# A filter transform as one float32 matmul per tile in place of three float32r matmuls

## The chip, the cores and the metric

The kernel runs on one core of a Trainium2 chip. Its metric is device time in microseconds (us), the median of several runs. The engines are TensorE (PE in the profile, its weight loads PEld), VectorE (DVE), ScalarE (ACT), GpSimd (POOL) and SyncE (SP), which issues nearly all transfers. Each executes its own instructions in order and waits on semaphores for the others.

## What is computed

One layer of an encoder for two sequences, of 512 and 2048 rows: a normalised input times w_in, three groups of heads (mLSTM, retention, Hyena), and a product with w_out. The change concerns the Hyena group's filters, which depend on the weights alone:

```python
hid = jnp.sin(fr * (feats @ w1 + b1))
hid = jnp.sin(fr * (hid @ w2 + b2))
filt = (hid @ w3).reshape(l, HY_ORDER, 2, HY_WIDTH)
filt = filt * jnp.exp(-t[:, :, None, None] * jnp.abs(deltas))
fwd, bwd = filt[:, :, 0], filt[:, :, 1]
two_sided = jnp.concatenate([fwd[:1] + bwd[:1], fwd[1:], jnp.zeros_like(fwd[:1]), jnp.flip(bwd[1:], axis=0)], axis=0)
two_sided = two_sided / jnp.sum(jnp.abs(two_sided), axis=0, keepdims=True)
spec = jnp.fft.rfft(two_sided, axis=0)
...
y = jnp.fft.irfft(jnp.fft.rfft(u, n=2 * l, axis=1) * spec[None], n=2 * l, axis=1)[:, :l]
```

The kernel does each Fourier transform of length 2l in two steps, over n1 and then over n2, each a matmul with a constant matrix.

## The kernel before

A float32 product of full accuracy is made here of three passes on parts: `split` writes hi, a copy of the source rounded to a narrower type, on ACT, and lo, the source less hi, on DVE (or POOL); `mm3` accumulates hi x hi, hi x lo and lo x hi in one PSUM tile. For the projections with w_in the parts are float16 (lines 540 and 550); for filters and transforms they are float32r, a type in which PE reads four bytes and makes a single pass (lines 372 to 374). The profile writes float32r operands of a matmul as f32, and as fp32r where ACT and DVE write them.

The filters come in two rounds, order 0 and order 1, of 40 tiles of 128x512 each (8 tiles for the short sequence, 32 for the long one). `filters(o)` is a loop over tiles n in which several steps of different tiles are put one behind the other: `first(n)` multiplies the hidden layer hd by w3 (three float32r matmuls into ps) and makes the window win on ACT; every fourth tile it also splits the next 128x512 of hd. `product(n)` writes f = ps x win on DVE. One turn later, `total` takes |f| on ACT and adds it to acc on POOL, and `second` splits f in f0 (ACT) and f1 (DVE). One turn after that, `third` multiplies by FA, the matrix of the DFT over n1 (three float32r matmuls), and `store` copies the result to fo on DVE and sends it to F in HBM. For the last tile of each filter (j = 0), `second` first adds a term for the skip to one row of f, which needs the finished sum acc (line 673) and so ends the chain of POOL. `filter_setup` loads the two FA matrices and splits them once.

The filter loop is a generator that is merged with others by planned costs: order 0 with the second half of the first Hyena projection, its gates and the end of the sine layers (`filter_mlp`, whose `h` is the first sine's result), order 1 with the Hyena projection of x1 and, on another stream, the Hyena transforms: `stage_a0` (parts hp, matrix ai) and `freq(0)` (parts hp, matrix cB, buffers hb). The generators give the program's sequence; a scheduler of the tile framework with its own simulated timeline then places the instructions of each engine. Tile pools set how many tiles of a name exist: f has FB = 1 buffer, win, fo, f0 and f1 have two. Line 660 is the product, 665 and 666 the sum, 694 the copy to fo; 365 and 366 are split's two rows for whatever tile, so tiles are told apart by name.

Of the kernel before, what the change touches and what calls it, by code (L numbers as in the profile page):

```python
# [10 lines left out]
F32R = mybir.dt.float32r  # L11
# [25 lines left out]

WK = 2
LF, LA, LI, LT, W1, W2, W3, LN, LM = 2.7, 2.5, 4.2, 1.6, 0.8, 1.08, 1.03, 1.5, 3.5
HB, HP, CB, FB, B1, B2, KA, KB, KC, LS2, WF, VB, FH = 9, 8, 3, 1, 5, 6, 3, 3, 1, 3, 70, 4, 8  # L40
R1, R2, R3, R4, M1, WG, W4, W5, W6 = 2.5, 2.0, 1.5, 0.6, 0.6, 60, 18, 11.5, 5.3


def geo(L):
    N = 2 * L
    N1 = N // 64
    V = N1 // 2
    return dict(N=N, N1=N1, K1=N1 // 2, V=V, GF=128 // N1, GS=128 // V, NTF=N // 128, NTS=L // 128)
# [98 lines left out]
class Trunk:  # L147
# [418 lines left out]
    def filter_setup(self):  # L566
        nc, C, p0 = self.nc, self.C, self.p0
        self.tneg = self.T(p0, [128, 40], "tneg", bufs=1)
        nc.sync.dma_start(self.tneg, C['tneg'])
        self.fa = {}  # L570
        for L in (LP, LS):
            self.fa[L] = [self.T(p0, [128, 128], f"FA{L}{i}", F32R, bufs=1) for i in range(2)]
            raw = self.T(p0, [128, 512], "fo")[:, 0:128]
            nc.sync.dma_start(raw, C[f'FA{L}'])
            self.split(*self.fa[L], raw)

    def filter_weights(self, o):
        nc, I, p0 = self.nc, self.I, self.p0
# [45 lines left out]
    def filters(self, o):  # L624
        nc, p0 = self.nc, self.p0
        w3, dl = self.filter_weights(o)
        tneg, fa = self.tneg, self.fa
        yield 3.0
        seq = [(L, 4 * b + t, t0 + 4 * b + t, i, t) for i, (L, b, t0) in enumerate(self.filter_blocks()) for t in reversed(range(4))]
        accs, hids, raws, st, sk = {}, {}, {}, {}, {}  # L630

        def fetch(i):
            raws[i] = self.T(p0, [128, 4, 128], "hd", bufs=1)
            nc.sync.dma_start(raws[i], self.hid[i].rearrange("p (t c) -> p t c", t=4))

        def first(n):
            L, j, jt, i, t = seq[n]
            if L not in accs:
                accs[L] = self.T(p0, [128, 512], "acc", bufs=1)
                nc.gpsimd.memset(accs[L], 0.0)  # L640
            if t == 3:
                if i == 0:
                    fetch(0)
                hids[i] = self.split(*(self.T(p0, [128, 4, 128], f"hd{x}", F32R, bufs=1) for x in range(2)), raws.pop(i))
                hids.pop(i - 1, None)
            if t == 2 and n + 4 < len(seq):
                fetch(i + 1)
            if j == 0:
                sk[L] = self.T(p0, [128, 512], "fo")[0:1]
                nc.sync.dma_start(sk[L], self.I['hy_skip'][:, o])  # L650
            ps = self.ps()
            self.mm3(ps, [x[:, t] for x in hids[i]], w3)
            win = self.T(p0, [128, 512], "win")
            nc.scalar.activation(win, dl, AF.Exp, scale=tneg[:, jt:jt + 1])
            st[n] = [ps, win]

        def product(n):
            ps, win = st[n]
            f = self.T(p0, [128, 512], "f", bufs=FB)
            nc.vector.tensor_tensor(out=f, in0=ps, in1=win, op=ALU.mult)  # L660
            st[n] = [f, win]

        def total(n):
            (f, win), acc = st[n], accs[seq[n][0]]
            nc.scalar.activation(win, f, AF.Abs)  # L665
            nc.gpsimd.tensor_tensor(out=acc, in0=acc, in1=win, op=ALU.add)  # L666

        def second(n):
            L, j, _, _, _ = seq[n]
            f, acc = st[n][0], accs[L]  # L670
            if j == 0:
                ps = self.ps()
                nc.tensor.matmul(ps[0:1], self.ones[:, 0:1], acc, start=True, stop=True)
                nc.vector.tensor_tensor(out=ps[0:1], in0=ps[0:1], in1=sk[L], op=ALU.mult)
                nc.vector.tensor_tensor(out=f[0:1], in0=f[0:1], in1=ps[0:1], op=ALU.add)
                ps = self.ps()
                for cb in range(4):
                    nc.tensor.matmul(ps[:, cb:cb + 1], acc[:, cb * 128:(cb + 1) * 128], self.ones[:, 0:1], start=True, stop=True)
                nc.vector.reciprocal(self.rs[L][:, o], ps[:, 0:4])
            else:  # L680
                total(n)
            st[n] = self.split(*(self.T(p0, [128, 512], f"f{x}", F32R) for x in range(2)), f)

        def third(n):
            L = seq[n][0]
            ps = self.ps()
            self.mm3(ps, fa[L], st[n])
            st[n] = ps

        def store(n):  # L690
            L, j, _, _, _ = seq[n]
            g = geo(L)
            fo = self.T(p0, [128, 512], "fo")
            nc.vector.tensor_copy(fo, st.pop(n))
            nc.sync.dma_start(self.F[L, o][:, j::g['NTF'], :], fo)

        n = len(seq)
        for i in range(n + 2):
            if i < n:
                first(i)  # L700
            if 0 <= i - 2:
                third(i - 2)
            if 0 <= i - 1 < n:
                if seq[i - 1][1] == 0:
                    total(i - 1)
                    yield self.lag(0.0, LS2, 1.28)
                second(i - 1)
            if 0 <= i - 2:
                store(i - 2)
            if i < n:  # L710
                product(i)
            yield self.lag(1.28, LT)
# [1022 lines left out]
```

## Time and profile before

| | |
|---|---|
| median of 3 runs | 2742.09 us (2740.89 to 2746.55) |
| the profiled execution's own time | 2752.46 us |
| its span, first to last instruction | 2750.7 us |
| PE busy (17,670 matmul records) | 2554.4 us, 93% |
| DVE busy | 1708.6 us, 62% |
| ACT busy | 1401.0 us, 51% |
| POOL busy | 758.2 us, 28% |
| mean granted clock of PE | 0.977 |

The busy times are of one profiled execution, whose time lies 10 us above the median. PE's matmuls overlap in the pipeline, so PE's busy time counts more than its work, and the distance from one start to the next says more about a matmul's price than its own duration does. The shares are means over stages that differ: the first filter round runs from about 157 to 404 us, the second to about 655 us, the Hyena transforms, further projections and retention to about 1690 us, and mLSTM and the output product behind that. The granted clock is a share of 2.4 GHz and has two levels, 2.4 and 1.2 GHz.

### The profile page before, as it was taken

The page shows a single profiled execution, that of the slowest core. Times are in us where ns is not written, and L with a number is a line of the kernel's source. Part 1 is how long each engine was busy: PE and PEld are TensorE (multiplying, and loading weights), DVE is VectorE, ACT ScalarE, POOL GpSimd, SP SyncE. Part 2 cuts the span into 40 slices and gives each one's busy share as a digit, 9 for nine tenths or more (in the row PEclk, how much of TensorE's full clock was granted, in tenths as well). Part 3 has the DMA queues.
Part 4 walks back from the last instruction along what each step waited for, and adds up shares of the span by engine and source line. Part 5 has one row for each costly group of instructions (what it writes and reads, how often), then busy time and mean ns, then how long its engine had stood idle before and what let it go on. Part 6 is the DMA issues. An engine that isn't in the chain of part 4 may idle for free.

```text
span 2750.7 us, 47623 instructions
## 1 busy us (share of the span) xinstructions
PE 2554.4 (93%) x17670; PEld 1927.4 (70%) x17670; DVE 1708.6 (62%) x3398; ACT 1401.0 (51%) x2710; POOL 758.2 (28%) x847
## 2 busy tenths in 40 slices
PE   7999979988998999988989998999999999899998
PEld 5556645544645788877777786787777877788887
DVE  7867768897786566576676666555566555622222
ACT  6456666765665465465665444445454455511111
POOL 0102322454453422355565443011011111100000
PEclk9999999989999999999999999999999999999999
DMA  5232266657757556466665666112232132333321
GB/s 199 81 110 85 92 188 199 198 175 193 198 161 211 159 185 200 129 176 176 176 178 159 174 210 192 36 36 66 48 68 56 36 87 64 111 123 107 104 94 55
DMA packets 266800, 364.28 MB, mean 132 GB/s; under 512 B 25382, under 2 KB 138814, under 8 KB 266568
## 3 DMA queue, kind: packets, MB, share of 16 engines
q1 hardware_dynamic: 266488, 360.98, 44.6%
q8 instruction: 139, 2.28, 0.4%
q14 instruction: 93, 0.76, 0.1%
q0 software_dynamic: 80, 0.26, 0.0%
HBM read 206.33 MB, written 112.89 MB: 116 GB/s over the span
## 4 chain that ended last, share of the span: by engine, by line
PE 39%; DMA 6%; DVE 6%; ACT 4%; issue 3%; POOL 2%; SPq 0%; DVEq 0%; POOLq 0%; ACTq 0%
PE ps L550 14%; PE ps L1286 12%; PE ps L540 5%; DMA rb<-rowd 2%; DMA hb<-hb 2%; DMA wraw<-in_w_in 1%; PE ps L1437 1%; PE ps L1274 1%; DMA hb<-Z 1%; PE ps L373 1%; PE ps L372 1%; PE ps L374 1%; PE ps L1509 1%; POOL hb L969 1%; ACT hp L365 1%
## 5 line engine op out<-in xcount | busy, mean ns | idle before, releaser
L550 PE MATMUL ps<-whi,h 128*128 128x256 f16 (+2 forms) x6080 | 936.0, 258 | 0.1
L550 PEld LDWEIGHTS <-h 128*128 128x128 f16 x9120 | 772.5, 98 | 142.4 <-issue 59.9
L550 PE MATMUL ps<-wlo,h 128*128 128x256 f16 (+2 forms) x3040 | 738.6, 258 | 5.1 <-DVE wlo L523 5.1
L540 PE MATMUL ps<-h,whi 128*128 128x512 f16 x1600 | 491.6, 385 | 4.2 <-ACT whi L522 4.2
L365 ACT ACTIVATE hp<-hb 128x512 fp32r<-128x512 f32 x360 | 217.4, 626 | 256.1 <-DVE hb L970 154.0
L540 PE MATMUL ps<-h,wlo 128*128 128x512 f16 x800 | 306.2, 383 | 0.0
L540 PEld LDWEIGHTS <-whi 128*128 128x128 f16 x1600 | 151.2, 99 | 185.5 <-issue 44.0
L366 DVE TENSOR_TENSOR hp<-hb,hp 128x512 fp32r<-128x512 f32 x280 | 217.9, 790 | 66.3 <-ACT hp L365 62.0
L1286 PE MATMUL ps<-h,yh 128*128 128x512 f32 x760 | 210.3, 396 | 1.6 <-ACT yh L365 1.6
L666 POOL TENSOR_TENSOR acc<-acc,win 128x512 f32<-128x512 f32 x80 | 109.4, 1367 | 215.4 <-ACT win L665 208.4
L1286 PEld LDWEIGHTS ps<-h,yh 128*128 128x128 f32 x760 | 141.7, 188 | 33.5 <-ACT yh L365 1.9
L366 POOL TENSOR_TENSOR hp<-hb,hp 128x512 fp32r<-128x512 f32 x80 | 114.6, 1432 | 167.2 <-ACT hp L365 158.8
L540 PEld LDWEIGHTS <-wlo 128*128 128x128 f16 x800 | 79.1, 99 | 95.6 <-issue 12.2
L969 POOL TENSOR_TENSOR hb<-hb,hb 128x512 f32<-128x512 f32 x80 | 113.0, 1412 | 113.2 <-DMA hb<-hb 75.5
L372 PE MATMUL ps<-hp,cB 128*128 128x512 f32 x240 | 113.3, 475 | 32.9 <-ACT hp L365 32.3
L366 DVE TENSOR_TENSOR f<-f,f 128x512 fp32r<-128x512 f32 x80 | 99.8, 1248 | 50.9 <-ACT f L365 50.8
L1617 POOL TENSOR_TENSOR m<-raw,tb 128x256 f32<-128x256 f32 x80 | 74.5, 931 | 183.8 <-ACT raw L1614 135.4
L1286 PE MATMUL ps<-h,yl 128*128 128x512 f32 x380 | 121.1, 396 | 0.0
L373 PE MATMUL ps<-hp,cB 128*128 128x512 f32 x240 | 107.0, 446 | 13.3 <-DVE hp L366 12.9
L968 DVE TENSOR_TENSOR hb<-hb,hb 128x512 f32<-128x512 f32 x80 | 68.3, 854 | 78.8 <-DMA hb<-hb 63.6
L802 DVE SCALAR_TENSOR_TENSOR cv<-u,sw,cv 128x512 f32<-128x512 f32 x120 | 110.5, 932 | 0.6
L1342 DVE TENSOR_TENSOR xt<-xt,ps 128x512 f32<-128x512 f32 x40 | 25.8, 684 | 126.9 <-PE ps L1286 126.9
(337 smaller groups left out, 5014.5 us busy)
## 6 DMA issues: line engine op xcount, KB each, us to landing
hb<-hb SPq DMA_DIRECT2D x316, 128.0 KB
F<-fo SPq DMA_DIRECT2D x80, 256.0 KB
Sg<-hb SPq DMA_DIRECT2D x80, 256.0 KB
hb<-Sg SPq DMA_DIRECT2D x80, 256.0 KB
hb<-F SPq DMA_DIRECT2D x80, 256.0 KB
Z<-hb SPq DMA_DIRECT2D x80, 256.0 KB
hb<-Z SPq DMA_DIRECT2D x80, 256.0 KB
rb<-rowd SPq DMA_DIRECT2D x80, 256.0 KB
```

Of the source, the lines that this page charges most:

```text
L365: self.nc.scalar.activation(hi, src, AF.Copy)
L366: (eng or self.nc.vector).tensor_tensor(out=lo, in0=src, in1=hi.bitcast(F32), op=ALU.subtract)
L372: mm(out, w[0], x[0], start=start, stop=False)
L373: mm(out, w[0], x[1], start=False, stop=False)
L540: nc.tensor.matmul(out, w[x][:, k, wc:wc + 128], self.hT[b][y][:, k], start=(k == 0 and i == 0), stop=(k == 7 and i == 2))
L550: nc.tensor.matmul(out, self.hT[b][x][:, k, c * 128:(c + 1) * 128], w[y][:, k, wc:wc + n], start=(k == 0 and i == 0), stop=(k == 7 and i = ...
L666: nc.gpsimd.tensor_tensor(out=acc, in0=acc, in1=win, op=ALU.add)
L802: nc.vector.scalar_tensor_tensor(d, u[:, t:t + 512], w(t), d, op0=ALU.mult, op1=ALU.add)
L968: nc.vector.tensor_tensor(out=x, in0=x, in1=fr, op=ALU.mult)
L969: nc.gpsimd.tensor_tensor(out=xs, in0=xs, in1=fi, op=ALU.mult)
L1286: self.nc.tensor.matmul(self.pss[n], a[p], w[q][:, n * 512:(n + 1) * 512], start=(k == 0 and i == 0), stop=(k == 11 and i == 2))
L1617: nc.gpsimd.tensor_tensor(out=m, in0=raw[:, :, ::-1], in1=sin[:, c:c + 2], op=ALU.mult)
```

## The change

`third` multiplies the tile f itself by FA in one float32 matmul. `second` no longer splits f, and `filter_setup` loads the FA matrices in their places and doesn't split them. f has three buffers in place of one, since it is now read by PE a turn later.

```diff
-HB, HP, CB, FB, B1, B2, KA, KB, KC, LS2, WF, VB, FH = 9, 8, 3, 1, 5, 6, 3, 3, 1, 3, 70, 4, 8
+HB, HP, CB, FB, B1, B2, KA, KB, KC, LS2, WF, VB, FH = 9, 8, 3, 3, 5, 6, 3, 3, 1, 3, 70, 4, 8
...
         for L in (LP, LS):
-            self.fa[L] = [self.T(p0, [128, 128], f"FA{L}{i}", F32R, bufs=1) for i in range(2)]
-            raw = self.T(p0, [128, 512], "fo")[:, 0:128]
-            nc.sync.dma_start(raw, C[f'FA{L}'])
-            self.split(*self.fa[L], raw)
+            self.fa[L] = self.T(p0, [128, 128], f"FA{L}", bufs=1)
+            nc.sync.dma_start(self.fa[L], C[f'FA{L}'])
...
-            st[n] = self.split(*(self.T(p0, [128, 512], f"f{x}", F32R) for x in range(2)), f)
+            st[n] = f
...
             ps = self.ps()
-            self.mm3(ps, fa[L], st[n])
+            nc.tensor.matmul(ps, fa[L], st[n], start=True, stop=True)
```

The planned costs stay as they were, but the scheduler places rows anew between the start of the filters and the first steps of the Hyena transforms behind them; later only a few neighbouring rows change places. Lines behind the edit have numbers smaller by two.

On PE, in the first round, at a tile for which hd has just been split (w is w3's part, hd the hidden layer's, FA the matrix, h the projection's input). Before:

```order
L372 MATMUL ps_2932<-w_361_1932,hd_564_2928 128x512
L373 MATMUL ps_2932<-w_362_1933,hd_564_2928 128x512
L372 MATMUL ps_2938<-f_559_2894,FA_358_1926 128x512
L373 MATMUL ps_2938<-f_560_2895,FA_358_1926 128x512
L374 MATMUL ps_2938<-f_559_2894,FA_359_1927 128x512
L550 LDWEIGHTS h_102
L550 MATMUL ps_2903<-wlo_1954,h_102 128x256
```

After:

```order
L372 MATMUL ps_2812<-w_357_1924,hd_522_2808 128x512
L373 MATMUL ps_2812<-w_358_1925,hd_522_2808 128x512
L374 MATMUL ps_2812<-w_357_1924,hd_523_2809 128x512
L685 MATMUL ps_2818<-f_2739,FA_356_1922 128x512
L550 LDWEIGHTS h_102
L550 MATMUL ps_2783<-whi_1945,h_102 128x256
```

Three rows with FA became one, and the third row with hd moved ahead of it.

On DVE, in the second round, around a split of hd (cv and wlo belong to projections, hp and hb to the Hyena transforms). Before:

```order
L366 TENSOR_TENSOR f_1332_5825<-f_5772,f_1331_5824 128x512
L660 TENSOR_TENSOR f_5831<-ps_5812,win_5816 128x512
L523 SCALAR_TENSOR_TENSOR wlo_5775<-wraw_3855,wsc_4146,whi_5774 128x512 x2
L694 COPY fo_5828<-ps_5818 128x512
L800 TENSOR_SCALAR cv_1297_5723<-u_1352_5906,sw_77_203 128x512
L802 SCALAR_TENSOR_TENSOR cv_1297_5723<-u_1296_5719,sw_77_203,cv_1297_5723 128x512
L366 TENSOR_TENSOR hd_1344_5876<-hd_5684,hd_1343_5875 128x512
L968 TENSOR_TENSOR hb_5734<-hb_5734,hb_5736 128x512
L802 SCALAR_TENSOR_TENSOR cv_1297_5723<-u_1352_5906,sw_77_203,cv_1297_5723 128x512
L694 COPY fo_5895<-ps_5885 128x512
L366 TENSOR_TENSOR f_1349_5892<-f_5831,f_1348_5891 128x512
```

After:

```order
L658 TENSOR_TENSOR f_5399<-ps_5386,win_5390 128x512
L523 SCALAR_TENSOR_TENSOR wlo_5349<-wraw_3613,wsc_3888,whi_5348 128x512 x2
L692 COPY fo_5396<-ps_5392 128x512
L366 TENSOR_TENSOR hd_1198_5444<-hd_5270,hd_1197_5443 128x512
L968 SCALAR_TENSOR_TENSOR hb_5314<-hb_5315,sgn_87,hb_5314 128x512
L798 TENSOR_SCALAR cv_1155_5303<-u_1204_5468,sw_77_203 128x512
L692 COPY fo_5457<-ps_5453 128x512
```

The rows that subtract f0 from f are gone, and hd's row stands ahead of cv's rows, not behind two of them.

On ACT, at the start of the filters (dl is the decay, u a projection, h the sine for the last hidden block, mhd its neighbour's). Before:

```order
L585 ACTIVATE dl_1935<-dl_1935 128x512
L654 ACT_TABLE_LOAD
L654 ACTIVATE win_2017<-dl_1935,tneg_1918 128x512
L564 ACT_TABLE_LOAD
L564 ACTIVATE mhd_1648<-sx_1570 64x4x64 x2
L654 ACT_TABLE_LOAD
L654 ACTIVATE win_2041<-dl_1935,tneg_1918 128x512
L365 ACTIVATE w_361_1932<-fo_1934 128x512
L789 ACTIVATE u_324_1678<-ps_1606,winv_165 128x512
L365 ACTIVATE hd_375_2009<-hd_2007 128x512
L564 ACT_TABLE_LOAD
L564 ACTIVATE h_318_1629<-sx_1628 64x512
```

After:

```order
L564 ACTIVATE mhd_1648<-sx_1570 64x4x64 x2
L365 ACTIVATE w_357_1924<-fo_1926 128x512
L583 ACTIVATE dl_1927<-dl_1927 128x512
L787 ACTIVATE u_324_1678<-ps_1606,winv_165 128x512
L365 ACTIVATE hd_371_2001<-hd_1999 128x512
L652 ACT_TABLE_LOAD
L652 ACTIVATE win_2009<-dl_1927,tneg_1918 128x512
L652 ACTIVATE win_2033<-dl_1927,tneg_1918 128x512
L564 ACT_TABLE_LOAD
L564 ACTIVATE h_318_1629<-sx_1628 64x512
```

mhd stands ahead of dl, the two rows of win follow each other, and between dl and h there are two table loads in place of four.

## Rows read from the trace of the kernel before

**Rows 1.** Busy us by stretch (records): PE, PEld, DVE, ACT, POOL; clock, DMA, GB/s

```profile
157.00:404.00 247.00, 222.40 (x1258) 141.84 (x1259) 170.86 (x237) 158.13 (x241) 61.92 (x72) 0.95 0.38 121
404.00:655.00 251.00, 221.10 (x939) 130.99 (x938) 213.71 (x280) 170.01 (x307) 107.38 (x108) 0.95 0.62 192
```

**Rows 2.** Waits of PE from 157 to 655 us: us, times, longest

```profile
PE ps L372 <- ACT hp L365: 9.4, 8, 3.0
PE ps L372 <- ACT hd L365: 8.6, 6, 2.4
PE ps L372 <- ACT f L365: 5.9, 5, 2.7
PE ps L372 <- issue: 5.6, 1, 5.6
PE ps L729 <- ACT h L564: 5.5, 1, 5.5
PE ps L374 <- DVE hd L366: 4.1, 3, 2.4
PE ps L373 <- DVE hp L366: 4.1, 4, 2.7
PE ps L373 <- DVE f L366: 3.9, 8, 1.3
```

**Rows 3.** Groups by line and form, 157 to 655 us: busy, mean ns, idle before

```profile
L366 DVE TENSOR_TENSOR f<-f,f 128x512 fp32r<-128x512 f32 x80 | 99.8, 1248 | 50.9 <-ACT f L365 50.8
...
L365 ACT ACTIVATE f<-f 128x512 fp32r<-128x512 f32 x80 | 49.4, 617 | 8.9 <-DVE f L675 8.9
```

**Rows 4.** Timeline of PE from 320 us: start, us, line, idle before

```profile
324.04 0.50 PE L372 MATMUL ps<-w,hd 128*128 128x512 f32 x1 [1.56 <-ACT hd L365]
...
324.61 0.40 PE L372 MATMUL ps<-f,FA 128*128 128x512 f32 x1
...
325.31 0.28 PE L550 MATMUL ps<-wlo,h 128*128 128x256 f16 x1
```

**Rows 5.** Timeline of PE, a float32 matmul of mLSTM and its successor

```profile
1782.79 0.39 PE L1437 MATMUL ps<-vw,kN 128*128 128x129 f32 x2
1783.01 0.27 PE L550 MATMUL ps<-whi,h 128*128 128x256 f16 x1
```

**Rows 6.** Timeline of PE, float32 matmuls of the first sine layer

```profile
92.88 1.93 PE L721 MATMUL ps<-ft,w 33*64 33x512 f32 x4
94.74 0.33 PE L436 MATMUL ps<-ident,xt 128*128 128x128 f32 x1
```

**Rows 7.** Timeline of PE, a float32 matmul of the second sine layer

```profile
82.78 0.27 PE L550 MATMUL ps<-wlo,h 128*128 128x256 f16 x1
82.89 0.27 PE L550 MATMUL ps<-whi,h 128*128 128x256 f16 x1
83.09 1.12 PE L729 MATMUL ps<-h,w 64*128 64x512 f32 x2
84.14 0.28 PE L550 MATMUL ps<-whi,h 128*128 128x256 f16 x1
```

**Rows 8.** Timeline of ACT ahead of the wait in rows 4

```profile
323.37 0.62 ACT L365 ACTIVATE hd<-hd 128x512 fp32r<-128x512 f32 x1
```

**Rows 9.** Timeline of DVE in the second round

```profile
579.36 1.16 DVE L366 TENSOR_TENSOR f<-f,f 128x512 fp32r<-128x512 f32 x1
...
585.30 1.75 DVE L366 TENSOR_TENSOR hd<-hd,hd 128x512 fp32r<-128x512 f32 x1
```

**Rows 10.** Timeline of ACT at the start of the filters

```profile
162.21 0.63 ACT L585 ACTIVATE dl<-dl 128x512 f32<-128x512 f32 x1 [3.95 <-DMA dl<-in_hy_deltas]
...
164.88 1.28 ACT L564 ACT_TABLE_LOAD   x1
166.18 0.84 ACT L564 ACTIVATE mhd<-sx 64x256 f32<-64x256 f32 x2
...
171.97 0.63 ACT L564 ACTIVATE h<-sx 64x512 f32<-64x512 f32 x1
```

## The prediction

> **What bounds the kernel now.** The change touches only the filter stages, so the first view to read is the table of busy time by stretch. The two rounds of filters run from 157 to 404 us and from 404 to 655 us; TensorE (PE) is busy for 222 of 247 and 221 of 251 us there, and VectorE (DVE) for 171 and 214 us [rows 1]. PE is the bound in both, but not a full one: about 26 and 30 us are idle, and the granted clock means 0.95, so that PE was at half clock for about a tenth of the time. In the second stretch DVE, with 85% busy, is nearly a bound of its own. The list of waits says what the idle PE waited for [rows 2]: the parts f0 and f1 of a filter tile (5.9 and 3.9 us), the parts of the hidden layer hd (8.6 and 4.1), the parts hp of the Hyena transforms (9.4 and 4.1), the sine layer h (5.5), and one wait of 5.6 us that the profile gives to no releaser. Together 47.1 us. All but the last are made on ScalarE (ACT) or DVE, whose load the change lowers. Behind 655 us nothing but the end of the Hyena steps moves, so what the two stretches win or lose goes to the end of the kernel unchanged.
>
> **What it removes.** Per tile, one ACT copy to float32r and one DVE subtraction: 80 copies of 617 ns, 49.4 us, and 80 subtractions of 1248 ns, 99.8 us [rows 3]. These engines aren't the chain by themselves, so none of that counts directly; it counts where PE waits for them. The setup copies of FA go too (they stand in a wait for a transfer and cost nothing).
>
> **What it adds on PE.** Three matmuls become one float32 matmul of the same 128x128 matrix and 512 columns. The three take 0.70 us from the first to the next line's start, 324.61 to 325.31 us [rows 4]. Before has no float32 matmul of exactly the new shape. What it has always appears as two records. Three neighbours price it:
> - On the full 128x128 array, with 129 columns, L1437 stands between float16 matmuls and takes 0.22 us, from 1782.79 to 1783.01 [rows 5]. Scaled to 512 columns that is 0.87 us, an estimate.
> - With 512 columns but 33 rows by 64 columns of weights, two matmuls in a row (four records) take 1.86 us, 92.88 to 94.74, so 0.93 each [rows 6].
> - With 512 columns and 64 rows of weights, alone between float16 matmuls, L729 takes 1.05 us to the next start, and starts 0.20 us after its predecessor, though two such predecessors start 0.11 us apart: 1.14 us in all [rows 7].
>
> I take 0.87, since it is the row with the full array that FA uses: 80 x (0.87 - 0.70) = +14 us. The upper end is 1.14: 80 x 0.44 = +35 us. It is the lower end too: [rows 6] less the 0.09 us by which L729 starts late [rows 7] is (1.86 - 0.09)/2, or 0.88.
>
> The Trainium skill, FP8 and Floating Point Precision, TensorE Precision Notes, speaks against the change: true float32 takes four passes through the array. Set against three passes at 0.70 us this would be 0.93 us, +19 us, and the sum below would end 5 us later; the 0.22 us of the full-array row [rows 5] lies nearer to the smaller price.
>
> **What the waits give back.** PE executes in order, so a wait that shrinks moves all that stands behind it.
> - *f, 9.8 us* [rows 2]: FA's matmul now reads the product itself, which DVE made two turns of the loop earlier. What remains is the last tile of each filter, where a row is added first. Taken: 8.5.
> - *hd, 12.7 us*: at 324.04 PE waited 1.56 us for ACT's copy of hd [rows 4]; ACT copies hd at 323.37, without idle time ahead of it [rows 8], in a queue that also holds a copy of f of 0.6 us for every tile. At 585 us it is DVE: none of its seven lines from 579 to 587 us has idle time ahead of it, f's subtraction of 1.16 us is one of them, and hd ends at 587.05 [rows 9]. Without f's rows hd comes 0.6 to 1.2 us earlier at least, and more where several of them stand in the queue. Taken: 9; between 4 and 12.7.
> - *hp, 13.5 us*: these are in the crowded part from 540 us on, behind the same queues, but also behind transfers that the change doesn't touch. Taken: 5; between 0 and 10.
> - *h, 5.5 us*: ACT reaches h at 171.97, after waiting until 162.21 for a transfer, with four table loads in between [rows 10]. In the new order two of these loads and mhd's row stand ahead or are gone: 2 x 1.28 + 0.84 = 3.4. Taken: 3.5.
> - *the 5.6 us without a releaser*: at the change of rounds ACT waits there for dl's transfer; still there. Taken: 0.
> - *clock*: 5% of 498 us is 25 us of granted clock missing. If some idle stretches go, part of it returns; taken 4, between 0 and 10.
>
> Sum: +14 - 8.5 - 9 - 5 - 3.5 - 4 = -16, and -17 with 1 us for the shorter waits of that list. The profiled execution of 2752.46 us (span 2750.7) would become about 2735; that execution is 10 us above the median of the three runs, so on the median 2742.09 the forecast is **2725 us**. Where f's splits were a cover for something, nothing is lost: no transfer waited for them. f keeps its buffer longer (until the matmul), which is what three buffers in place of one provide; with one, the product of the next tile would stand on DVE behind PE, and ACT and the sum on GpSimd (POOL) behind it.
>
> **Rivals.** *The waits form again elsewhere* (A). PE comes earlier to the Hyena steps, whose data come over queues that are 0.62 busy in the second stretch [rows 1]; the hd and hp waits then stay as long in total. Only f and h return: +14 - 12 = +2, 2744 us. For it: hp's is the longest line of the list already. Against it: ACT and DVE do get 149 us of work less [rows 3].
>
> *The matmul costs what L729 does* (B). Place: each of the 80 FA matmuls stands between float32r and float16 work, as L729 stands between float16 work. At 1.14 us [rows 7] it costs +35; the waits return 27, the clock nothing: +8, 2750 us, slower. It decides from 0.70 + 27/80 = 1.04 us a tile. Against it: L1437 is just as isolated and shows 0.22 us for 129 columns, without such a rim [rows 5]. The Trainium skill, TensorEngine Tiling (Array Packing), Key Properties, says that a change of tiling mode drains TensorE; by that rule the rim belongs to L729's 64 rows and not to float32, and FA, with the whole array before and after, would not pay it. No row of before shows FA in float32.
>
> *DVE was the true bound of the second stretch* (C). For it: its 214 us of 251 [rows 1]. Then the waits go to their upper ends, 9.8 + 12.7 + 10 + 5.5, with the clock's 10, less PE's 14: -34; with the 5.6 us at the change of rounds and shorter waits about -42, 2700 us. Against it: in the first stretch DVE has a third of its time free.
>
> That the change isn't done is no rival: the new order has 160 fewer matmuls on PE and 80 fewer rows for f on ACT and DVE.
>
> **How the numbers follow.** Forecast 0.57 (2725; its own range 2708 to 2738), A 0.17 (2744), B 0.13 (2750), C 0.13 (2700). The range for 8 in 10 goes from C's time to B's, 2700 to 2750. About 0.2%, 5.5 us, is what a measurement of this kernel can tell from no change, so faster means below 2736.6: nearly all of the forecast's case and C, 0.67. Within: most of A and the forecast's edge, 0.17. Slower: B and A's upper side, 0.16.
>
> **What would show it.** In the changed kernel's profile the FA line should have 160 records in place of 240, and 0.87 us from its first record to the next instruction's start; 1.1 or more is B. The waits of PE for f should be gone, for hd below 5 us, and for h near 2. DVE should have about 100 us less in the two stretches, and the second filter round should end 10 us or more earlier. If hd's and hp's waits are as long as before while DVE's load fell, it is A. The forecast is wrong if the second round ends later than 655 us, or if PE's price and the waits are right and the time is given back behind it.

## The result, and the profile after

The changed kernel takes 2702.4 us (median of four runs, 2697.2 to 2704.1) where the kernel before, beside it, takes 2741.5; the ratio is 0.9846, with a 95% interval of 0.9832 to 0.9859. That is 39 us less. The forecast was 2725, 17 us less: the sign and the range hold, but the gain is more than twice what was forecast. The profiled execution has a span of 2702.3 us, so it may stand for the median; that of before lay 10 us above its own.

Where the time went is read from two marks that both traces have. The last row with FA on PE starts at 648.6 us before and at 621.6 after. The last transposes of cv (line 835, now 833), near where the moved rows end, start at 875.1 and 840.9. So 27 us are won by the end of the filter rounds and 34 by the second mark. A tile's view gives its rows' count, the shortest, median and longest duration in ns, and the first and the last start. The kernel before:

```profile
L373 PE MATMUL ps<-f,FA x80: 387/478/795, 205.1 to 648.4; 128*128 128x512 f32 x80
L374 PE MATMUL ps<-f,FA x80: 388/397/628, 205.3 to 648.6; 128*128 128x512 f32 x80
...
L835 PE MATMUL ps<-ident,cv x240: 270/281/454, 47.3 to 875.1; 128*128 128x128 f32 x120
```

The changed kernel:

```profile
L685 PE MATMUL ps<-f,FA x160: 590/592/1057, 202.1 to 621.6; 128*128 128x512 f32 x160
...
L833 PE MATMUL ps<-ident,cv x240: 270/277/460, 47.3 to 840.9; 128*128 128x128 f32 x120
```

The float32 matmul is two records, 160 for 80 tiles. Its price stands in the timeline of PE (start, us, line, idle before):

```profile
302.22 0.39 PE L374 MATMUL ps<-w,hd 128*128 128x512 f32 x1
302.45 1.02 PE L685 MATMUL ps<-f,FA 128*128 128x512 f32 x2
303.31 0.27 PE L550 MATMUL ps<-whi,h 128*128 128x256 f16 x1
```

From 302.45 to the next start at 303.31 it takes 0.86 us, and it starts 0.23 us after its predecessor, so it has no rim as the neighbour with 64 rows has in [rows 7].

The waits of PE in the two rounds, to be set beside [rows 2] (us, times, longest):

```profile
PE ps L372 <- ACT hp L365: 14.0, 7, 4.5
PE ps L727 <- ACT h L564: 3.1, 1, 3.1
PE ps L372 <- ACT w L365: 2.7, 1, 2.7
PE ps L685 <- DVE sw L761: 2.5, 1, 2.5
PE ps L372 <- ACT hd L365: 2.1, 2, 1.5
PE ps L374 <- DVE hd L366: 1.5, 1, 1.5
```

The waits for f0 and f1 are gone but for one at the end of a filter; those for hd fell from 12.7 to 3.6 us. hp's line is longer because the wait at the change of rounds, which had no releaser before, is counted in it now (5.1 us of the 14.0). The whole list of these two rounds falls from 54 to 28 us.

The table of stretches answers [rows 1]; its columns are busy us (records) of PE, PEld, DVE, ACT and POOL, then the clock:

```profile
157.00:384.00 227.00, 217.36 (x1207) 138.58 (x1208) 130.76 (x194) 133.37 (x196) 59.32 (x72) 0.97 0.40 128
384.00:623.00 239.00, 220.86 (x888) 125.22 (x886) 168.21 (x233) 148.20 (x265) 105.27 (x107) 0.95 0.65 207
```

PE is busy for 438 of 466 us now, where it was 443 of 498. The plainest change is on DVE. Its groups, before (mean ns of one, then the idle time ahead of them and what ended it):

```profile
L660 DVE TENSOR_TENSOR f<-ps,win 128x512 f32<-128x512 f32 x80 | 54.7, 684 | 5.1 <-PE ps L374 1.7 <-DVE f L366 0.5
```

and after:

```profile
L658 DVE TENSOR_TENSOR f<-ps,win 128x512 f32<-128x512 f32 x80 | 54.7, 687 | 66.7 <-PE ps L374 47.2 <-ACT u L787 7.6 <-ACT win L652 6.6
```

Before, the product hardly ever waited for PE: DVE was late, since it stood 50.9 us ahead of f's subtractions until ACT had copied f [rows 3]. After, DVE waits 47.2 us for PE. The two engines changed roles.

### The profile page after: what moved, and what is told of

Its sections match the earlier page's. It is cut to its first block, busy times and chain, and to the rows that moved or that the text cites. A ratio compares the mean times of both kernels' runs of the same rounds, so it can differ in the third digit from the quotient of the medians.

```text
span 2702.3 us, 47221 instructions
## 1 busy us (share of the span) xinstructions
PE 2550.8 (94%) x17590; PEld 1918.7 (71%) x17590; DVE 1624.9 (60%) x3316; ACT 1355.3 (50%) x2626; POOL 758.4 (28%) x847
## 4 chain that ended last, share of the span: by engine, by line
PE 62%; DMA 9%; DVE 9%; ACT 7%; issue 4%; POOL 2%; SPq 1%; POOLq 0%; DVEq 0%; ACTq 0%
PE ps L550 21%; PE ps L1284 12%; PE ps L540 11%; DMA rb<-rowd 3%; PE ps L372 3%; DMA hb<-hb 2%; PE ps L373 2%; PE ps L374 2%; PE ps L685 2%; DVE hb L968 1%; ACT hp L365 1%; POOL hb L967 1%; PE ps L1435 1%; PE ps L1272 1%; DMA hb<-Z 1%
## 5 line engine op out<-in xcount | busy, mean ns | idle before, releaser
L968 DVE SCALAR_TENSOR_TENSOR hb<-hb,sgn,hb 128x512 f32<-128x512 f32 x80 | 81.6, 1020 | 38.6 <-POOL hb L967 35.5
L1349 POOL TENSOR_TENSOR ss<-ss,mhalf 128x1 f32<-128x1 f32 x20 | 10.9, 543 | 331.4 <-DVE ss L1348 328.8
```

What stands on the lines that cost most here:

```text
L968: nc.vector.scalar_tensor_tensor(x, xs, self.sgn, x, op0=ALU.mult, op1=ALU.add)
```

## Experiments

Each variant was timed beside the kernel before on its own chip, whose medians lay between 2746 and 2750 us; so variants are compared by their ratios, and 0.001 is 2.7 us. The scheduler places rows anew in each of them.

**The two kernels again.** `before_again`:

> The kernel before, profiled a second time. The profiled execution of before lay 10 us above the median, and its stretch behind the filter rounds (655 us to the end) took 16 us longer than the same work in the changed kernel. If that is the one execution: the stretch behind the filter rounds is 8 to 14 us shorter here, and the two rounds still take 497 to 499 us. If it is an effect of the change: the stretch is as long as before, and the lower time comes from the filter rounds.

The filter rounds are the same to 1 us. The execution took 2748.4 us, and from the last transposes (875.2) to the end of its span (2746.6) there are 1871 us, against 1876 in the first profile. So only 4 us of it were that execution. `after_again`:

> The changed kernel once more, as the base for the runs beside it on the same chip: 2697 to 2708 us. The stretch behind the last mixing transposes of the Hyena convolution took 1861 us in its first profile and 1871 to 1876 in two profiles of before. If the change gains nothing there, this profile lies anywhere between 1861 and 1875; if it does, near 1861 again.

2708.5 us beside 2749.6: the ratio is 0.9851 (0.9835 to 0.9867), the same gain of 41 us. The end took 1865 us (843.1 to 2708.3), the first time 1861. The kernel before is the slower one here, but the two variants of the changed kernel in which only a planned cost differs (below) lie at 1860 and 1878. In all twenty profiles of this document, this end takes 1870 to 1882 us where f is split for the product (five profiles, 1875 in the mean) and 1858 to 1878 us in the others (fifteen, 1866), though its rows hardly change. So some 7 of the 41 us probably come from that part; no run tells why. A whole time thus varies by up to 20 us with something behind the filter rounds. The second mark is steadier: two profiles of the kernel before reach it at 875.1 and 875.2 us, two of the changed kernel at 840.9 and 843.1.

**Load or dependency.** `both_splits_kept` puts both operations back, read by nobody; `act_copy_kept` and `dve_sub_kept` one of them:

```diff
+            self.split(*(self.T(p0, [128, 512], f"f{x}", F32R, bufs=1) for x in range(2)), f)
             st[n] = f
```

```diff
+            nc.scalar.activation(self.T(p0, [128, 512], "f0", F32R), f, AF.Copy)
```

```diff
+            nc.vector.tensor_tensor(out=self.T(p0, [128, 512], "f1", F32R), in0=f, in1=f, op=ALU.subtract)
```

> The changed kernel with f0 and f1 still written for every tile (ACT copy and DVE subtraction, one buffer each), and read by nobody; PE does the float32 matmul on f. So ACT and DVE carry the load of before, and PE no longer waits for the parts. Relief theory (most of the gain is that ACT and DVE have 149 us less to do, and hd, hp, acc come earlier): only FA's own waiting goes, -14, against +13 for the matmul, so about 2740 us, nearly all of the 39 us lost. Rival, the dependency: the gain is that PE no longer stands behind the parts of f, and the engines' load does not matter: 2702 to 2710 us.

> The changed kernel with f0 alone still written for every tile (ACT copy of 0.62 us), read by nobody. DVE is relieved of 100 us, ACT of nothing. If DVE's load (85% busy in the second round) is what delays hd, hp and the rest: about 2712 us. If ACT's is (its waits are the longer lines of the list, 14.5 us of hd and hp against 8.2 on DVE): about 2726 us. Dependency theory: 2702 to 2708 us.

> The changed kernel with a DVE subtraction of f's size still made for every tile (f less f, result read by nobody), and no ACT copy. ACT is relieved of 49 us, DVE of nothing. If DVE's load is what counts: about 2730 us. If ACT's is: about 2714 us. Dependency theory: 2702 to 2708 us.

Measured: 2730.8 us with both (ratio 0.9942, 0.9922 to 0.9961), 2720.9 with ACT's copy (0.9906, 0.9882 to 0.9930), 2710.2 with DVE's subtraction (0.9864, 0.9835 to 0.9892). Against 0.985 for the changed kernel, the two splits cost 25 us, ACT's alone 15, DVE's alone 4. So the load of the splits is worth some 25 us, and both theories fall by half: the dependency alone leaves 16 us of gain, where the relief theory expected about none. Some of the 25 us may be the variant's own: f0 and f1 have one buffer each in it, where before has two, and ACT stands 11.2 us for DVE's subtraction ahead of its copies. ACT's 49 us seem to count more than DVE's 100; the two intervals touch, but at the second mark too the variants stand at 853.9 and 847.3 us. With ACT's copy and nobody waiting for it, PE's wait for ACT's w is 4.9 us in place of 2.7, and hp's is 16.6 in place of 14.0 (waits of PE from 157 to 633 us):

```profile
PE ps L372 <- ACT hp L365: 16.6, 6, 5.9
PE ps L372 <- ACT w L365: 4.9, 1, 4.9
```

The whole list grows by 7 us, so about half of ACT's 15 us isn't traced to a wait of PE.

**The buffers of f.** `one_f_buffer` is the changed kernel with FB = 1, `both_splits_one_buffer` is both_splits_kept with FB = 1, so that the load and f's one buffer are those of before and the matmul differs. Two things more differ from before: f0 and f1 have one buffer each in place of two, and f is held a turn longer, until the matmul has read it. The edit of both:

```diff
-HB, HP, CB, FB, B1, B2, KA, KB, KC, LS2, WF, VB, FH = 9, 8, 3, 3, 5, 6, 3, 3, 1, 3, 70, 4, 8
+HB, HP, CB, FB, B1, B2, KA, KB, KC, LS2, WF, VB, FH = 9, 8, 3, 1, 5, 6, 3, 3, 1, 3, 70, 4, 8
```

> The changed kernel with one buffer for f as before. The product of a tile then waits on DVE for the matmul of the tile ahead, and ACT and POOL stand behind it. My theory: the two copies more are needed, 8 to 20 us are lost, about 2715 us. Rival: the matmul of tile n-1 stands well ahead of the product of tile n+1 in the program, so one buffer is enough: 2700 to 2706 us.

> both_splits_kept with one buffer for f as before: the load of ACT and DVE and the buffers of before, and only the three float32r matmuls replaced by one in float32 that reads f. Three buffers were worth 10 us in the changed kernel. If the parts add up: 2731 + 10 = 2741 us, so that the matmul alone, +13 for PE and -14 for the waits for f0 and f1, brings nothing. Rival: the matmul's own swap already brings the 15 us that both_splits_kept has below before, 2731 us.

Measured: 2718.8 us (0.9891, 0.9876 to 0.9905) and 2752.1 us (1.0019, 1.0007 to 1.0031). The two buffers more are worth 11 us without the splits and 21 with them, and the matmul with the splits and one buffer is 5 us slower than the kernel before, where 2741 or 2731 us were expected. The second mark (here in line 834 or 833) says the same of the buffers, in both_splits_one_buffer, both_splits_kept and one_f_buffer:

```profile
L834 PE MATMUL ps<-ident,cv x240: 270/277/454, 48.5 to 893.9; 128*128 128x128 f32 x120
L834 PE MATMUL ps<-ident,cv x240: 270/277/459, 49.2 to 864.6; 128*128 128x128 f32 x120
L833 PE MATMUL ps<-ident,cv x240: 270/277/455, 47.7 to 854.9; 128*128 128x128 f32 x120
```

There the buffers are worth 29 us with the splits and 12 to 14 without, and the matmul with the splits and one buffer costs 19, most of which this profile's shorter end (1861 us) hides in the whole time. These marks are of one profile each. In both_splits_one_buffer PE's waits for f0 and f1 are replaced by one for the product itself, and the sum on POOL comes late (waits of PE from 157 to 674 us):

```profile
PE ps L686 <- DVE f L658: 31.9, 17, 4.4
PE ps L671 <- POOL acc L664: 14.3, 2, 9.1
```

The ring behind this can be read in the kernel before, on DVE from 319 to 327 us:

```profile
319.59 0.69 DVE L660 TENSOR_TENSOR f<-ps,win 128x512 f32<-128x512 f32 x1
320.20 0.68 DVE L694 COPY fo<-ps 128x512 f32<-128x512 f32 x1
321.50 1.41 DVE L366 TENSOR_TENSOR f<-f,f 128x512 fp32r<-128x512 f32 x1 [0.62 <-ACT f L365]
323.01 0.69 DVE L660 TENSOR_TENSOR f<-ps,win 128x512 f32<-128x512 f32 x1
323.62 0.68 DVE L694 COPY fo<-ps 128x512 f32<-128x512 f32 x1
324.21 0.68 DVE L366 TENSOR_TENSOR hd<-hd,hd 128x512 fp32r<-128x512 f32 x1
327.09 1.41 DVE L366 TENSOR_TENSOR f<-f,f 128x512 fp32r<-128x512 f32 x1 [2.19 <-ACT f L365]
```

and on ACT:

```profile
320.32 0.63 ACT L665 ACTIVATE win<-f 128x512 f32<-128x512 f32 x1 [0.62 <-DVE f L660]
320.86 0.61 ACT L365 ACTIVATE f<-f 128x512 fp32r<-128x512 f32 x1
...
324.00 1.28 ACT L654 ACT_TABLE_LOAD   x1
...
326.44 0.61 ACT L365 ACTIVATE f<-f 128x512 fp32r<-128x512 f32 x1
```

The product (319.59) is read by ACT for |f| (320.32) and for f0 (320.86); only then can DVE subtract (321.50), and only then is the one buffer free for the next product (323.01). Each turn crosses between DVE and ACT twice, and DVE, which executes in order, stands for what ACT has in its queue: at 327.09 for 2.19 us, until the copy of f that ACT starts at 326.44, with a table load of 1.28 us ahead of it.

**The subtraction on POOL.** `low_part_on_pool` is the kernel before with another engine for f1:

```diff
-            st[n] = self.split(*(self.T(p0, [128, 512], f"f{x}", F32R) for x in range(2)), f)
+            st[n] = self.split(*(self.T(p0, [128, 512], f"f{x}", F32R) for x in range(2)), f, eng=nc.gpsimd)
```

> The kernel before, still with three float32r matmuls, and f1 subtracted by POOL in place of DVE. DVE is relieved of the 100 us of subtractions and of the 51 us in which it stood behind ACT's copies f0; ACT, PE and the one buffer stay. If DVE standing there is what made hd, hp and the products late: 10 to 20 us less than before, 2728 to 2738 us. If ACT's load is (13 to 16 us came back with the copies alone), or if POOL, with the sum in its queue, delivers f1 late: 2744 to 2760 us.

2760.1 us (1.0043, 1.0026 to 1.0060), slower by 12 us. DVE is not relieved of standing there: it waits for POOL ahead of the next product now (waits of DVE from 157 to 670 us),

```profile
DVE f L660 <- POOL f L366: 61.1, 30, 4.4
```

and PE for f0 (waits of PE):

```profile
PE ps L372 <- ACT f L365: 45.4, 29, 4.1
```

Moving the subtraction keeps the ring and makes one step of it slower; so the run doesn't tell DVE's standing from ACT's load, and it agrees with the ring as the cause. The direct test, the kernel before with its three float32r matmuls and three buffers for f, wasn't tried; with one buffer each for f0 and f1, as in both_splits_kept, it would need five tiles for the three names, as before does. So what before's one buffer costs by itself is argued from the trace and from the neighbouring variants.

**PE's price.** `matmul_twice` makes the product with FA twice, `three_passes` and `three_passes_clean` make it in 0.70 us, `one_pass` in 0.24:

```diff
             nc.tensor.matmul(ps, fa[L], st[n], start=True, stop=True)
+            nc.tensor.matmul(ps, fa[L], st[n], start=True, stop=True)
```

```diff
-            f = self.T(p0, [128, 512], "f", bufs=FB)
+            f = self.T(p0, [128, 512], "f", F32R, bufs=FB)
...
-            nc.tensor.matmul(ps, fa[L], st[n], start=True, stop=True)
+            for k in range(3):
+                nc.tensor.matmul(ps, fa[L], st[n], start=k == 0, stop=k == 2)
```

The first edit is matmul_twice's, the second that of three_passes_clean, without its rounding of FA. three_passes_clean adds the same product up three times, and three_passes counts the product with FA's high part twice, so both give a time alone and not the transform.

> The changed kernel with the float32 matmul made twice into the same tile, each from its own start, so the result stays. 80 more of them at 0.86 us are 69 us of PE. PE theory: about 2771 us. If the waits that are left (28 us listed in the two rounds) take in part of it, because data come while PE works: 2745 to 2760 us.

> The changed kernel with f written as float32r by the product and multiplied in three float32r passes (FA's two parts, f where its low part stood), nothing split per tile. It leaves out the low part of f. ACT, DVE and the buffers are as in the changed kernel, PE has 0.70 us a tile in place of 0.86. PE theory (what PE needs counts 1:1): 13 us less than the changed kernel, about 2690 us. Rival, PE is no longer what sets these stretches: no difference, 2700 to 2705 us.

> The changed kernel with f and FA as float32r and the matmul as three passes of the same two operands (0.70 us in place of 0.86). FA is rounded once by POOL, so ACT's and DVE's queues are those of the changed kernel, unlike in three_passes. It leaves out the low parts of f and FA. If PE sets the two rounds 1:1: 13 us less than the changed kernel beside three_passes (2708.5), 2695 us. If the data set them and PE's work fits beside: at most 4 us less, 2704 to 2709 us.

> As three_passes_clean with a single float32r pass, 0.21 us a tile in place of 0.86: 80 x 0.65 = 52 us of PE's work less, all else as in the changed kernel. If PE sets the rounds 1:1: 2656 us. If the data set them: 2685 to 2700 us, with hp's and hd's waits longer by what PE saves.

Measured: 2767.7 us (1.0064, 1.0043 to 1.0084); 2715.6 (0.9877, 0.9860 to 0.9894); 2710.8 (0.9871, 0.9849 to 0.9893); 2679.6 (0.9752, 0.9731 to 0.9773). Doubling adds 69 us of work and 59 of time. 50 us less (80 x (0.86 - 0.24)) give 27 us, so that one_pass ends between its two expectations. 13 us less give nothing in either form; three_passes_clean reaches the second mark at 840.3 us, where the changed kernel has 840.9 and 843.1. From one pass to two matmuls, 118 us of work are 86 us of time, 0.7 of each. The rest is taken up at both ends: in matmul_twice PE no longer waits for ACT's hp, and its clock over the two rounds is 0.99, where after_again has 0.96 (157 to 674 and 157 to 625 us, columns as above). First matmul_twice:

```profile
157.00:674.00 517.00, 497.92 (x2257) 290.47 (x2255) 296.32 (x428) 288.79 (x463) 166.44 (x177) 0.99 0.49 152
```

then after_again:

```profile
157.00:625.00 468.00, 442.05 (x2106) 265.98 (x2104) 302.77 (x430) 283.45 (x464) 165.06 (x180) 0.96 0.53 168
```

In three_passes_clean, PE's saving went into waits. Those for hp and hd are longer than in after_again, where hp has 12.1 us and hd 3.6 (waits of PE from 157 to 622 us):

```profile
PE ps L372 <- ACT hp L365: 17.4, 7, 7.1
PE ps L374 <- DVE hd L366: 4.3, 1, 4.3
...
PE ps L372 <- ACT hd L365: 2.5, 3, 1.5
```

**What placement alone does.** Four runs change the planned cost of a filter tile, and no work:

```diff
-            yield self.lag(1.28, LT)
+            yield self.lag(1.24, LT)
```

> The kernel before with the planned cost of a filter tile at 1.24 in place of 1.28: nothing is computed otherwise, and rows of the filter rounds change places. How much the placement alone moves the time: if little, 2742 to 2752 us, as before; if the placement of before was a poor one, 10 to 20 us less.

> As before_plan_1_24 with 1.30. If the placement alone moves little: 2742 to 2752 us. If it is worth 10 us and more, the difference between variants of the change below that size say nothing about PE or the queues.

> The changed kernel with the planned cost of a filter tile at 1.24: 2704 to 2712 us if placement alone moves little. If it moves 10 us, the missing 13 us of three_passes_clean may be placement, and not that the data set these rounds.

> As after_plan_1_24 with 1.30: 2704 to 2712 us if placement alone moves little; a spread of 10 us or more between the two and the changed kernel if it does not.

Before: 1.0002 (0.9990 to 1.0014) with 1.24 and 1.0044 (1.0027 to 1.0062) with 1.30. Changed: 0.9838 (0.9822 to 0.9854) and 0.9911 (0.9892 to 0.9929). The cost of 1.24 is worth nothing to 4 us, that of 1.30 loses 12 and 17 us. So the change gains 37 to 45 us under each of three plans, and its effect is no accident of placement. But a single difference of some 10 us between variants can be: the missing 13 us of three_passes_clean, ACT's 15 us against DVE's 4, and the exact split between buffers and load are not settled by whole times. The 17 us lie behind the rounds: after_plan_1_30 reaches the second mark at 838.8 us, earlier than the changed kernel, and takes 1878 us from there. At that mark the three plans of the changed kernel spread from 834 to 843 us, those of before from 873 to 879.

**Versions that go further.** `early_loads` fetches the second round's weights and decays in the middle of the first; `one_pass_early` does that in one_pass:

```diff
+            if o == 0 and i == n // 2:
+                self.filter_loads(1)
```

> The changed kernel with the weights and decays of the second round fetched in the middle of the first (dl with two buffers, w3's raw tile in its own). It takes away ACT's wait of 5.4 us for dl's transfer at the change of rounds, behind which PE waits 4.5 us for hp and 3.3 us for w. If that wait is what ends late there: 5 to 8 us less, 2701 to 2704 us on the chip of the runs before. If something else is late at once: 2706 to 2709 us.

> one_pass with the loads of early_loads. It leaves out the low parts of f and FA. one_pass had 2679.6 us, early_loads 8 to 10 us less than the changed kernel. If the two add: 2671 us. If hp's wait at the change of rounds gives way to another: 2677 to 2681 us.

early_loads: 2698.6 us (0.9824, 0.9799 to 0.9849), 7 us less than the changed kernel by the ratios, though the intervals overlap. In its list of waits ACT no longer waits for dl, and hp has 8.0 us in place of 12.1 in after_again. one_pass_early: 2672.7 us (0.9743, 0.9706 to 0.9779), the lowest median of all, but its interval covers that of one_pass. one_pass and one_pass_early give up precision, since they leave out the low parts; of the versions that compute in full, early_loads has the lowest median, below both kernels.

## Why the prediction was wrong in size

- **PE's term held as a price.** 0.86 us a tile against 0.87 forecast, 80 x 0.16 = +13. The neighbour with the full array was the right one, and rival B (1.14) has no support: no rim shows. The Trainium skill (FP8 and Floating Point Precision, TensorE Precision Notes) has four passes for true float32; the trace agrees if a pass is that of a float16 matmul with as many columns, two of which start within 0.43 us (last section), since four of them are 0.86, the measured price. The prediction took a third of 0.70 for a pass and so came to 0.93; a float32r pass, 0.24 in one_pass, costs a little more than a float16 one. Whether the whole 13 us reach the end is open: over a wider span 0.7 of PE's work did.
- **f, hd and h held as listed waits.** f went from 9.8 to 2.5 us (forecast 8.5 back, 7.3 came), hd from 12.7 to 3.6 (9 and 9.1), h from 5.5 to 3.1 (3.5 and 2.4). hp without the change of rounds went from 13.5 to 8.9 on ACT's line with 0.7 on POOL's (5 and 4). The 5.6 us at the change of rounds stayed, as forecast, since ACT waits there for dl; early_loads shows that part of them was to be had.
- **The step that failed is the last one of the part on the waits, that the buffers are only what the later reading of f needs.** It entered the sum with nothing. That the later reading needs them is right: in one_f_buffer DVE's product stands 73.8 us for PE's matmul. But they bring more than that back. By ratios, the change with one buffer is 30 us below before (at the second mark 20), where the forecast had 17 for the whole; the two further buffers bring another 11 (at the mark 12 to 14). In another order of the same steps, the float32 matmul with one buffer and the splits is +5 us (forecast +14 - 8.5 = +5.5, by luck: the waits are other ones than it named, and at the mark it is +19), three buffers are -21 (forecast 0), and leaving out the splits is -25 (forecast -9 - 5 - 3.5 - 4 - 1 = -22.5). Either sum is -41 where the forecast had -17, so the buffers are 11 to 21 of the 24 us that it lacked. The rest is in the splits, worth 25 us with three buffers and 35 with one. Placement may move each of these by some 10 us; that the buffers gain is seen in both pairs, by the ratios and at the mark.
- **A premise failed with it, that what the two stretches win goes to the end unchanged.** 34 us are won at the second mark and 39 to 41 at the end. The end behind the mark is 9 us shorter in the mean of the profiles; why stays open.
- **Why the view did not show it.** The prediction summed what PE's list of waits names. Counted over all of PE's records, from start to start, less one cycle a column at the granted clock (two in each record of a float32 matmul), PE lost 103 us in the two rounds before and 59 after: 44 us, of which the list names 26. Of the other 18, about 5 lie at the starts that the list names and the rest at starts where it names nothing; some 5 of the 18 are in the price already, since three passes took 0.70 us for 0.64 us of columns (3 x 512 at 2.4 GHz). Those that the list names but the prediction passed over count too: POOL's sum acc, 3.7 us before, is gone.
- **The row that told it stood in [rows 3].** DVE's 50.9 us of idle time ahead of f's subtractions, ended by ACT, were read as free time, since DVE was not the chain by itself. Rival C was set aside because DVE has a third of its time free in the first stretch. That time was not free: DVE stood in it with the next product behind. C's time of 2700 is nearly what was measured, but its mechanism, DVE's load, is not it: the load alone (dve_sub_kept) costs 4 us. What the runs show is the buffers and the load of the splits, of ACT's copy more than of DVE's subtraction; that before's ring between DVE and ACT is behind it is read from the trace.
- **Rival A fell**: hp's waits, the change of rounds included, went from 19.1 to 14.7 us and hd's nearly away. That waits can form again when PE gets faster shows in three_passes_clean.
- **The clock's term held**: 0.95 in both stretches before, 0.97 and 0.95 after. By the forecast's own way of counting, 25 us of granted clock were missing in the two rounds before and 19 after, so 6 us came back where 4 were taken.
- **One reading was off and carries nothing**: PE's idle time in the first stretch is 25 us (247.0 - 222.4), where the prediction has 26.

## What to carry to other kernels

Where a tile has one buffer and its readers sit on two engines, read the ring (who must have read before the next may be written) and count the in-order engine's idle time inside it as busy. A list of waits names only the long ones: compare what an engine loses between its starts with the sum of that list before you price a relief by it. And when a change drops an operation, ask which buffers that sets free; here they were a quarter to a half of the gain.

## What the runs showed of the hardware

A float32 matmul of the full array with 512 columns is two records and takes 0.86 us from its start to the next instruction's, against 0.70 for three float32r passes (timeline of PE in three_passes_clean) and 0.24 for one (the same in one_pass):

```profile
300.98 0.85 PE L688 MATMUL ps<-f,FA2048r 128*128 128x512 f32 x3
301.68 0.28 PE L550 MATMUL ps<-whi,h 128*128 128x256 f16 x1
```

and

```profile
302.01 0.40 PE L687 MATMUL ps<-f,FA2048r 128*128 128x512 f32 x1
302.25 0.28 PE L550 MATMUL ps<-wlo,h 128*128 128x256 f16 x1
```

Two float16 matmuls of 512 columns take 0.43 us (the same in the changed kernel), so one takes 0.215, and the float32 matmul four times that:

```profile
300.22 0.59 PE L540 MATMUL ps<-h,whi 128*128 128x512 f16 x2
300.65 0.38 PE L540 MATMUL ps<-h,wlo 128*128 128x512 f16 x1
```

More float32 work on PE went with a higher granted clock: 0.96 over the two rounds with one matmul a tile, 0.99 with two, with fewer waits ahead of PE as well; which of the two did it was not tried. And DVE's subtraction f less f0 has two durations, 0.68 and 1.41 us: of the 80 before, 21 last under 0.8 us and have POOL at work for under a tenth of their time, 54 last over 1.3 us and have it for about 70%. No run moved that alone.
